# Middle stores of a one-core hybrid decoder step issued by GpSimd, g0 written in one transfer, and one round of background visits instead of three

## The chip, the cores and the metric

The kernel runs on one core of a Trainium2 chip. The metric is the device time of one execution in microseconds. The engines are TensorE (PE), VectorE (DVE), ScalarE (ACT), GpSimd (POOL) and SyncE (SP). Each works through its own instructions in order. Loads and stores run on 16 DMA engines; an instruction on SP's, ACT's or POOL's queue issues them.

## The reference

One inference step of a two-layer decoder, for a prompt of 512 positions and a sample group of 8 sequences of 8 positions, 576 columns in all, model width 2048:

```
layer 0: h = rms_norm(x); q,k,v,z_a,b,c,h_in,z_b = split(h @ w_in_ab, 8)
  prompt attention: 8 heads x 128, three dilated causal windows merged
  sample attention: the same against a cache of 2048 keys and values per sequence
  mixer B: b * conv3(c * h_in);  y = concat(o_a * silu(z_a), o_b * silu(z_b)) @ w_out_ab
layer 1: u,z = split(rms_norm(x) @ w_in_c, 2)
  S5: 128 groups, 16 channels, 64 complex states, chunked scan, Re(C h) + D u
  y = gelu(y); y = y * sigmoid(y @ w_glu + b); out = x + (y * silu(z)) @ w_out_c
final rms_norm; new keys, values, conv and SSM states are outputs too
```

All arithmetic is fp32. Main products split both operands into a high and a low fp32r part and use three products of the four.

## The kernel before

**Main work.** There are 120 jobs in a fixed order: 0 to 23 the heads' q, k and v columns, 24 to 31 z_a, 32 to 63 the convolution's columns, 64 to 67 the output projection, 68 to 99 u and z, 100 to 115 the GLU, 116 to 119 the last projection. A job of the narrow kind (all but 64 to 67 and 116 to 119) has 96 main matmuls of 288 columns, in eight groups of 12. Weights come as 512 KB tiles `w` from SP's queue; ACT makes the high part `wh`, DVE the low part `wl` (`wl = w - wh`), and the matmuls write PSUM tiles `mm`, of which there are two.

**Background work.** Everything else is a Python generator, a *thread*. A thread yields what its next step waits for (an engine, tiles, free buffers, a condition) and goes on when it is resumed. The order of all instructions is written out once, when the program is built, by a planner: class `Clock` adds up an estimated time for each engine and each DMA, and `could` says whether a thread's next step would be ready by that estimate. Before each group of 12 main matmuls `between` calls `step`; in this text that is a **visit**. A visit first lets evacuations of PSUM go on (`evacs`, as far as they can), and then goes round the threads in order of priority, each one step, up to three rounds. A step for an engine that is planned over 3.5 us ahead is not taken. Where the main work can go no further (`until`), `force` resumes the thread that is ready first, with no main matmuls beside it. Since an engine keeps its order, an instruction that was planned too early holds up all that stand behind it.

**The stretches.** `prompt_heads` runs the eight heads one after another, 24 steps and a condition each; a head can begin when its three jobs are done. Beside it `ssm_setup` prepares the state-space layer and starts `ssm_x` (16 chunks: load tiles E and B, DVE makes X, store to bx_scr) and `ssm_c` (16 chunks: transposes tx, tile XY, DVE makes Cs, matmuls gp with B0, stores to cs_scr, and for each two chunks g0 in tile gsb to gz_scr). X, Cs and gsb have one buffer each. `heads_done` is asked from job 24 on, and from job 29 on it is forced (`until(heads_done)` in `hook2`). Then `open_sample` starts the sample attention: `near_load` and `far_load` bring cache tiles kv and kf (512 KB each), `sample_far` works on DVE with kf, and `sample_near` goes through four pairs of sequences, 54 steps a pair: 20 for keys (tkn, sps), 11 to the softmax (nw, tf, tp), 21 for values (os), and two for the output. When it is done, `fill_o` splits the stored columns of o_scr for the output projection; `hook3` forces that at job 64. In layer 1 `v_phase`, `scans`, `y_phase`, `gelus` and `final_states` run beside jobs 68 to 99, and `fill_y` (38 steps) must be done for job 100.

**Queues around the change.** Loads are issued on SP. Stores of the middle of the program are issued on ACT, next to ACT's activations: the heads' k, v and q, oa_scr and o_scr, bx_scr, cs_scr, gz_scr, the convolution states, h_scr, z_scr and the final SSM states. An issue waits on the issuing queue until its tile is complete. POOL has some memsets, the copies into qz (for each sample pair) and into HV (for each scan), and two small loads at the start. The planner counts 370 ns for an issue on any engine and a landing 3200 ns after the data.

Of the kernel before, what the change touches and what calls it, by code (L numbers as in the profile page):

```python
# [10 lines left out]
F32 = mybir.dt.float32  # L11
# [7 lines left out]
P = 128  # L19
D = 2048  # L20
KT = 16
NP = 512
# [7 lines left out]
G = 128  # L30
GC = 16
ST = 64
# [46 lines left out]
class Clock:  # L79
# [91 lines left out]
    def op(self, eng, op, a, k):  # L171
        aps = [(n, x) for n, x in list(enumerate(a)) + list(k.items()) if hasattr(x, "tensor")]
        outs = [x for n, x in aps if n in (0, "out", "accum_out")]
        ins = [x for n, x in aps if n not in (0, "out", "accum_out")]
        by = "DMA" if op == "dma_start" else eng
        t = max([self.when(x, False, by) for x in ins] + [self.when(x, True, by) for x in outs])
        if op == "dma_start":
            at = max(self.t[eng], t) + 370
            self.t[eng] = at
            n = int(np.prod(outs[0].shape))  # L180
            run = min(self.packets(x, x.tensor.name in self.row) for x in outs + ins)
            self.dma = max(self.dma, at) + n / run * (5 + 0.2 * run) / 16
            end = max(self.dma, at) + 3200
        else:
            at = max(self.t[eng], t + 60)
            two = op != "memset" and sum(x.tensor.name in self.sbuf for x in ins) > 1
            shared = two if eng == "DVE" else eng == "POOL" and op != "memset"
            if shared:
                at = max(at, self.port)
            end = at + self.cost(eng, op, outs, ins)  # L190
            if eng == "PE":
                fast = op == "matmul" and ins[0].dtype == F32R
                if fast and not self.exact:
                    end += 85
                self.exact = fast
            self.t[eng] = end
            if shared:
                self.port = end
            if eng == "PE":
                end += 170  # L200
        for x in ins:
            self.note(x, end, False, by)
        for x in outs:
            self.note(x, end, True, by)
# [74 lines left out]
def hybrid_step(tc, I, O):  # L279
# [26 lines left out]
    _, cp = pools.open("const")  # L306
    _, wp = pools.open("wstream")
# [26 lines left out]
    e_scr = dr.tile([T, G, P], F32, name="e_scr")  # L334
    b_scr = dr.tile([GC, G, P], F32, name="b_scr")
    q_scr = dr.tile([64, 1024], F32, name="q_scr")
    gz_scr = dr.tile([G, GC, 240], F32, name="gz_scr")
    m0_scr = dr.tile([P, G, P], F32, name="m0_scr")
    bx_scr = dr.tile([P, G, P], F32, name="bx_scr")
    cs_scr = dr.tile([P, G, P], F32, name="cs_scr")  # L340
# [94 lines left out]

    def step():
        evacs()
        for _ in range(3):
            again = False
            for th in list(bg):  # L440
                if th in bg and could(th, 3500.0):
                    run(th)
                    again = True
                    evacs()
            if not again:
                return
# [452 lines left out]
    def ev_za(h, ps):  # L899
        yield W("DVE", ps)  # L900
        zs, th, gt = evt(2), evt(3), evt(0)
        mul(half(zs), ps, half(rstd))
        yield W("ACT", zs, flag=lambda: h in za_in)
        act(th, zs, AF.Tanh, scale=0.5)
        ob = za_in.pop(h)
        yield W("DVE", th, ob)
        stt(gt, th, 1.0, zs, ALU.add, ALU.mult)
        stt(ob, ob, 0.5, gt[:, 0:NP], ALU.mult, ALU.mult)
        yield W("ACT", ob)
        act(gs[:, h, :], gt[:, NP:])  # L910
        ACT.dma_start(out=o_scr[h, :, 0:NP], in_=ob)

    def load_oa():
        for h in range(NH):
# [14 lines left out]
    def prompt_head(h):  # L929
# [51 lines left out]
            PE.transpose(tk[:, i, :], k[:, i * P:(i + 1) * P], ident)  # L981
        kt_ = pp.tile([P, 4, P], F32, name="ktok", tag="PT", bufs=2)
        act(kt_, tk)
        ACT.dma_start(out=kout[:, h, :].rearrange("(i p) d -> p i d", p=P), in_=kt_)
        yield W("ACT", S[0][1])
        ex(0)
        yield w_qk(1)
# [8 lines left out]
            PE.transpose(tv_[:, i, :], v[:, i * P:(i + 1) * P], ident)  # L996
        vt_ = pp.tile([P, 4, P], F32, name="vtok", tag="vtok", bufs=2)
        act(vt_, tv_)
        ACT.dma_start(out=vout[:, h, :].rearrange("(i p) d -> p i d", p=P), in_=vt_)
        yield w_qk(2)  # L1000
        qk(2)
        yield W("DVE", S[1][0])
# [8 lines left out]
        sq = pp.tile([64, 2, P], F32, name="sq", tag="sq", bufs=1)  # L1011
        act(sq, tq[:, 0:2, :])
        DVE.tensor_copy(vs[:, h * P:(h + 1) * P], tq[:, 2, :])
        ACT.dma_start(out=q_scr[:, h * P:(h + 1) * P], in_=sq[:, 0, :])
        ACT.dma_start(out=ksout[:, h, :], in_=sq[:, 1, :])
        ACT.dma_start(out=vsout[:, h, :], in_=vs[:, h * P:(h + 1) * P])
        yield w_tr(0)
        tr(0)
        yield w_qk(3)
# [23 lines left out]
        yield W("ACT", o, slot=[(pp, "PT", 1)])  # L1043
        ob = pp.tile([P, NP], F32, name="ob", tag="PT", bufs=2)
        act(ob, o)
        ACT.dma_start(out=oa_scr[h], in_=ob)
        hs["done"] = h + 1


# [2 lines left out]
    def ssm_setup():  # L1052
# [15 lines left out]
        DVE.memset(pw[:, 0, 0, :], 1.0)  # L1068
        DVE.memset(pw[:, 0, 2, :], 1.0)
        for a in range(2):  # L1070
            SP.dma_start(out=gz_scr[:, :, 56 * a:56 * a + 56], in_=pw[:, 0, 1, 0:56].unsqueeze(1).to_broadcast([P, GC, 56]))
        yield W("ACT", lam, stp)
        lr, li = lam[:, 0, :], lam[:, 1, :]
        act(stp, stp, AF.Exp)
# [118 lines left out]
    def ssm_x(sp):  # L1193
        for c in range(G // CH):
            g0 = c * CH
            yield W("SP", e_scr, b_scr, slot=[(sp, "E8", 1), (sp, "B8", 1)])
            E = sp.tile([P, CH, 2, ST], F32, name="E8", tag="E8", bufs=1)
            B = sp.tile([P, CH, 2, ST], F32, name="B8", tag="B8", bufs=1)
            SP.dma_start(out=E.rearrange("p g a s -> p (g a s)"), in_=e_scr[:, g0:g0 + CH, :]
                         .rearrange("t g p -> t (g p)").unsqueeze(1).to_broadcast([T, GC, CH * P]))  # L1200
            SP.dma_start(out=B.rearrange("p g a s -> p (g a s)"), in_=b_scr[:, g0:g0 + CH, :]
                         .rearrange("k g p -> k (g p)").unsqueeze(0).to_broadcast([T, GC, CH * P]))
            er, ei, br, bi = E[:, :, 0, :], E[:, :, 1, :], B[:, :, 0, :], B[:, :, 1, :]
            yield W("DVE", E, B, slot=[(sp, "X8", 1)])
            X = sp.tile([P, CH, 2, ST], F32, name="X8", tag="X8")
            for a, (p, q, f) in enumerate(((br, bi, sub), (bi, br, add))):
                tb = sp.tile([P, CH, ST], F32, name="tb8", tag="tb8")
                mul(tb, ei, q)
                mul(X[:, :, a, :], er, p)
                f(X[:, :, a, :], X[:, :, a, :], tb)  # L1210
                if a == 0:
                    yield W("DVE")
            yield W("ACT", X)
            ACT.dma_start(out=bx_scr[:, g0:g0 + CH, :], in_=X.rearrange("p g a s -> p g (a s)"))
        st_["x"] = True
        ssm_end()

    def ssm_c(sp, B0, PWT):
# [13 lines left out]
        for c in range(G // CH):  # L1232
# [24 lines left out]
            for q in range(2):  # L1257
                for gi in range(4):
# [1 line left out]
                    PE.matmul(gp[32 * gi:32 * gi + 32, q, :], B0[:, (g0 + g) * GC:(g0 + g) * GC + 32],  # L1260
                              Cs[:, g, 0:8, :].rearrange("p t k -> p (t k)"), start=True, stop=True,
                              tile_position=(0, 32 * gi))
            ACT.dma_start(out=cs_scr[:, g0:g0 + CH, :], in_=Cs[:, :, 1:9, :].rearrange("p g t k -> p g (t k)"))
            if c % 2 == 0:
                gs_["t"] = sp.tile([P, 4, P], F32, name="gsb", tag="gsb")
            gsb = gs_["t"]
# [2 lines left out]
                stt(gsb[:, 2 * (c % 2) + q, 0:GC], eye, dsk[:, 2 * c + q:2 * c + q + 1], gp[:, q, 0:GC], ALU.mult, ALU.add)  # L1269
            if c % 2:  # L1270
                yield W("ACT", gsb)
                for gi in range(4):
                    ACT.dma_start(
                        out=gz_scr[(c - 1) * CH:(c + 1) * CH].rearrange("(q gi) k j -> gi k q j", gi=4)[gi][:, :, 112:240],
                        in_=gsb[32 * gi:32 * gi + GC])
        st_["c"] = True
        ssm_end()

# [6 lines left out]
    def m0_expand():  # L1285
        for t in range(T):
            yield W("SP", flag=lambda: cnt["i"] >= 4 * 64 + 6 * t)
            SP.dma_start(out=m0_scr[t * GC:(t + 1) * GC],
                         in_=gz_scr[:, :, GC * t:GC * t + P].rearrange("g k j -> k g j"))


    cvs = {}
# [1 line left out]
    def ev_conv(n, ps):  # L1294
# [32 lines left out]
        elif kind == 2:  # L1327
# [6 lines left out]
            nv = pp.tile([32, P], F32, name="ncv", tag="ncv")  # L1334
            act(nv[0:18, :], tl[0:18, :])
            js = slice(j * P, (j + 1) * P)
            ACT.dma_start(out=O["conv_p"][0, 0][:, js], in_=nv[0:2, :])
            ACT.dma_start(out=O["conv_s"][0].rearrange("b i f -> (b i) f")[:, js], in_=nv[2:18, :])
        else:
            yield W("DVE", ps)  # L1340
            zs, th, ob = evt(0), evt(1), evt(2)
# [9 lines left out]
            if "t" in Bt:  # L1351
                yield from split_B(8 + j, ob)
            else:
                ACT.dma_start(out=o_scr[8 + j], in_=ob)
                stored.append(8 + j)

    stored = list(range(8))
# [80 lines left out]
    def sample_near():  # L1438
# [115 lines left out]
            DVE.tensor_scalar(out=osb, in0=o, scalar1=st[:, 2:3], scalar2=None, op0=ALU.mult)  # L1554
            yield from sample_out(pr, osb)
        yield W("ACT", sa["oS"])
        ACT.dma_start(out=o_scr[0:8, :, NP:].rearrange("h p n -> p h n"), in_=sa["oS"])
        sa["done"] = True

    def open_sample():  # L1560
# [30 lines left out]
    def ev_out0(part, g, acc, tiles):  # L1591
# [15 lines left out]
        for i, n, h, x in got:  # L1607
            yield W("ACT", h)
            act(x, h, AF.Square, accum_out=ssqa[0:n, 4 * i + g:4 * i + g + 1])
            h1["xc"] += 1  # L1610
            ACT.dma_start(out=h_scr[i * P:i * P + n, g * 512:(g + 1) * 512], in_=h)

    def joined(ps):

# [81 lines left out]
    def ev_z(n, ps):  # L1696
        yield W("DVE", ps)
        zs, th = evt(1), evt(2)
        mul(half(zs), ps, half(h1["rstd"]))
        yield W("ACT", zs)  # L1700
        act(th, zs, AF.Tanh, scale=0.5)
        yield W("DVE", th)
        stt(th, th, 1.0, zs, ALU.add, ALU.mult)
        yield W("ACT", th)
        ACT.dma_start(out=z_scr[n], in_=th)

    w_c = I["w_in_c"][0]
    add_jobs(w_c, [m * P for m in range(16)], actA, ev_u)
# [170 lines left out]
    def final_states():  # L1879
# [3 lines left out]
        for src, re_out, im_out in outs:  # L1883
# [3 lines left out]
            f = sp.tile([G, P], F32, name="fo", tag="sn", bufs=3)  # L1887
            act(f, t)
            yield W("ACT", f)
            ACT.dma_start(out=re_out, in_=f[:, 0:ST])  # L1890
            ACT.dma_start(out=im_out, in_=f[:, ST:P])
        ss["fo"] = True

    def open_ssm():
# [327 lines left out]
```

## Time and profile before

| | us |
|---|---|
| median of 3 runs | 2350.19 |
| lowest, highest | 2349.2, 2360.9 |
| profiled execution | 2350.44 |
| its span, first to last instruction | 2348.5 |

Mean granted clock of TensorE over the span: 0.974. In the profile, busy times and idle times are in microseconds. In a list of instructions, "x" is their number. An idle time names the engine's own gap before the instruction and, after "<-", what ended it. A "q" behind an engine's name (ACTq) means its queue's own instruction, such as the issue of a DMA. PEclk is the granted share of TensorE's full clock of 2.4 GHz; the other level is 1.2 GHz. A DMA share of 1.0 means that all 16 DMA engines are busy.

### The profile page before, as it was taken

Reading aid. Unit: us, or ns where it says so; the run is one execution under the profiler, and the core shown is the slowest. Engines: PE = TensorE matmul, PEld = TensorE weight load, DVE = VectorE, ACT = ScalarE, POOL = GpSimd, SP = SyncE. Lnnn points to the kernel's source line nnn. Section 1 sums busy time; section 2 is a strip of 40 time slices with the busy share of each in tenths; the row PEclk is TensorE's granted clock in tenths of the full one; section 3 lists DMA queues with packets and bytes.
Section 4 is the critical chain, followed back from the end, with each engine's and each line's share of the span. In section 5 each row is a group of like instructions: output and inputs, shape, how many; then the busy total and the mean of one; then the engine's idle time right before and its main releaser. Section 6 shows DMA issues by size and latency. Waiting matters only on the chain.

```text
span 2348.5 us, 38368 instructions
## 1 busy us (share of the span) xinstructions
PE 2206.3 (94%) x15581; PEld 2034.7 (87%) x15581; DVE 1264.8 (54%) x2380; ACT 695.8 (30%) x1400; POOL 13.5 (1%) x52
## 2 busy tenths in 40 slices
PE   6998888899888989999999999999999999999997
PEld 5997777798676868899988789999999999998885
DVE  3776676746575644343323334787996534443333
ACT  4543333332121222232223333222233322332222
POOL 0000000000000000000000000000000000000000
PEclk9999999999898999999999999999999999999999
DMA  6466666659999987732246535465555643338212
GB/s 170 112 170 179 176 174 179 177 180 254 261 284 216 287 227 217 212 113 80 84 153 187 158 112 158 128 204 156 175 168 163 188 120 102 107 110 214 88 63 81
DMA packets 421796, 386.62 MB, mean 165 GB/s; under 512 B 34620, under 2 KB 349860, under 8 KB 420276
## 3 DMA queue, kind: packets, MB, share of 16 engines
q1 hardware_dynamic: 369552, 340.63, 52.6%
q10 hardware_dynamic: 52004, 43.53, 6.0%
q8 instruction: 122, 2.00, 0.4%
q14 instruction: 54, 0.44, 0.1%
q0 software_dynamic: 64, 0.02, 0.0%
HBM read 329.22 MB, written 63.28 MB: 167 GB/s over the span
## 4 chain that ended last, share of the span: by engine, by line
PE 70%; DMA 15%; DVE 9%; ACT 3%; issue 2%; SPq 1%; ACTq 0%; DVEq 0%
PE mm L215 59%; DMA kv<-cache_win_v 4%; DMA kf<-cache_win_k 3%; PE mms L215 3%; DVE m L215 2%; PE yps L215 2%; DMA B<-b_scr 2%; DMA out_win_k_p<-ktok 1%; PE os L215 1%; DVE wl L215 1%; DMA oa<-oa_scr 1%; SPq L215 1%; DMA w<-w_in_ab 1%; PE vps L215 1%; PE tkn L215 1%
## 5 line engine op out<-in xcount | busy, mean ns | idle before, releaser
L215 PE MATMUL mm<-a_hi,wh 128*128 128x288 f32 x3072 | 695.1, 308 | 5.7 <-ACT a_hi L215 5.7
L215 DVE TENSOR_TENSOR wl<-w,wh 128x512 fp32r<-128x512 f32 x576 | 392.3, 688 | 545.4 <-ACT wh L215 529.0
L215 PE MATMUL mm<-a_hi,wl 128*128 128x288 f32 x3072 | 666.5, 299 | 12.6 <-DVE wl L215 12.6
L215 PE MATMUL mm<-a_lo,wh 128*128 128x288 f32 x3072 | 666.3, 299 | 0.4 <-DVE a_lo L215 0.3
L215 ACT ACTIVATE wh<-w 128x512 fp32r<-128x512 f32 x576 | 357.3, 627 | 719.0 <-PE mm L215 363.5
L215 PEld LDWEIGHTS mm<-a_hi,wh 128*128 128x128 f32 x3072 | 502.5, 193 | 43.9 <-issue 28.1
L215 PEld LDWEIGHTS mm<-a_hi,wl 128*128 128x128 f32 x3072 | 502.4, 192 | 13.6 <-DVE wl L215 13.6
L215 PEld LDWEIGHTS mm<-a_lo,wh 128*128 128x128 f32 x3072 | 503.4, 192 | 1.2 <-DVE a_lo L215 1.2
L215 PE MATMUL mm<-y_hi,wh 128*128 128x288 f32 x512 | 109.7, 296 | 0.0
L215 PE MATMUL mm<-y_lo,wh 128*128 128x288 f32 x512 | 109.6, 296 | 0.0
L215 PE MATMUL mm<-y_hi,wl 128*128 128x288 f32 x512 | 109.6, 296 | 0.0
L215 PE MATMUL mm<-wh,a_hi 128*128 128x512 f32 x256 | 100.0, 391 | 1.9 <-DVE Y L215 1.9
L215 DVE TENSOR_TENSOR kf<-kf,qr 128x1024 f32<-128x1024 f32 x48 | 58.6, 1221 | 79.3 <-DMA kf<-cache_win_k 79.3
L215 PE MATMUL mm<-wh,o_hi 128*128 128x512 f32 x256 | 100.5, 393 | 0.0
L215 PE MATMUL mm<-wl,o_hi 128*128 128x512 f32 x256 | 99.7, 389 | 0.0
L215 PE MATMUL mm<-wh,o_lo 128*128 128x512 f32 x256 | 99.7, 389 | 0.0
L215 PE MATMUL mm<-wh,a_lo 128*128 128x512 f32 x256 | 99.6, 389 | 0.0
L215 PE MATMUL mm<-wl,a_hi 128*128 128x512 f32 x256 | 99.6, 389 | 0.0
L215 PEld LDWEIGHTS mm<-y_hi,wh 128*128 128x128 f32 x512 | 82.5, 189 | 0.0
L215 PEld LDWEIGHTS mm<-y_lo,wh 128*128 128x128 f32 x512 | 82.5, 189 | 0.0
L215 PEld LDWEIGHTS mm<-y_hi,wl 128*128 128x128 f32 x512 | 82.5, 189 | 0.0
L215 DVE TENSOR_TENSOR m<-HV,AT 64x256 f32<-64x256 f32 (+5 forms) x120 | 67.8, 565 | 3.6 <-ACT HV L215 1.2
(290 smaller groups left out, 2343.9 us busy)
## 6 DMA issues: line engine op xcount, KB each, us to landing
w<-w_in_ab SPq DMA_DIRECT2D x128, 512.0 KB
kv<-cache_win_v SPq DMA_DIRECT2D x80, 512.0 KB
w<-w_in_c SPq DMA_DIRECT2D x64, 512.0 KB
kf<-cache_win_k SPq DMA_DIRECT2D x48, 512.0 KB
kv<-cache_win_k SPq DMA_DIRECT2D x32, 512.0 KB
w<-w_out_ab SPq DMA_DIRECT2D x32, 512.0 KB
w<-w_glu SPq DMA_DIRECT2D x32, 512.0 KB
w<-w_out_c SPq DMA_DIRECT2D x32, 512.0 KB
```

The costliest lines, as they stand in the source:

```text
L215: r = f(*a, **k)
```

## The change

Stores that ACT issued are issued by POOL, with the planner counting 900 ns in place of 370 ns for an issue on POOL. The stores of y_scr and those of the last outputs stay on ACT. gz_scr has 32 rows a group in place of 16, so that the 128 partitions of gsb go out in one transfer and not in four; readers take the first 16. `step` goes round the threads once.

```diff
-            at = max(self.t[eng], t) + 370
+            at = max(self.t[eng], t) + (370 if eng != "POOL" else 900)
...
-    gz_scr = dr.tile([G, GC, 240], F32, name="gz_scr")
+    gz_scr = dr.tile([G, 32, 240], F32, name="gz_scr")
...
     def step():
         evacs()
-        for _ in range(3):
+        for _ in range(1):
...
-        ACT.dma_start(out=kout[:, h, :].rearrange("(i p) d -> p i d", p=P), in_=kt_)
+        POOL.dma_start(out=kout[:, h, :].rearrange("(i p) d -> p i d", p=P), in_=kt_)
...
-            ACT.dma_start(out=bx_scr[:, g0:g0 + CH, :], in_=X.rearrange("p g a s -> p g (a s)"))
+            POOL.dma_start(out=bx_scr[:, g0:g0 + CH, :], in_=X.rearrange("p g a s -> p g (a s)"))
...
-            ACT.dma_start(out=cs_scr[:, g0:g0 + CH, :], in_=Cs[:, :, 1:9, :].rearrange("p g t k -> p g (t k)"))
+            POOL.dma_start(out=cs_scr[:, g0:g0 + CH, :], in_=Cs[:, :, 1:9, :].rearrange("p g t k -> p g (t k)"))
...
-                for gi in range(4):
-                    ACT.dma_start(
-                        out=gz_scr[(c - 1) * CH:(c + 1) * CH].rearrange("(q gi) k j -> gi k q j", gi=4)[gi][:, :, 112:240],
-                        in_=gsb[32 * gi:32 * gi + GC])
+                POOL.dma_start(out=gz_scr[(c - 1) * CH:(c + 1) * CH].rearrange("(q gi) k j -> (gi k) q j", gi=4)[:, :, 112:240],
+                               in_=gsb)
```

The same move from ACT to POOL is made for the stores of o_scr, vout, q_scr, ksout, vsout, oa_scr, conv_p, conv_s, h_scr, z_scr and the final SSM states. The two readers of gz_scr take `0:GC` of its rows.

## Rows read from the trace of the kernel before

**Rows 1.** The page, part 1: busy time of each engine.

```profile
PE 2206.3 (94%) x15581; PEld 2034.7 (87%) x15581; DVE 1264.8 (54%) x2380; ACT 695.8 (30%) x1400; POOL 13.5 (1%) x52
```

**Rows 2.** Windows, main matmuls alone: length, busy (count), PEclk, DMA share, GB/s.

```profile
482.90:503.60 20.70, 17.06 (x109) 14.91 (x109) 1.15 (x2) 0.00 (x0) 1.00 0.27 75
516.00:972.30 456.30, 304.99 (x2058) 286.42 (x2057) 16.33 (x29) 0.00 (x0) 0.95 0.96 252
801.00:895.00 94.00, 58.79 (x397) 54.22 (x396) 3.14 (x6) 0.00 (x0) 0.98 0.93 254
972.30:1183.50 211.20, 211.20 (x1582) 210.90 (x1583) 12.64 (x24) 0.00 (x0) 1.00 0.35 103
1017.00:1119.40 102.40, 102.40 (x768) 102.26 (x767) 6.32 (x12) 0.00 (x0) 1.00 0.30 86
1811.40:1920.50 109.10, 107.25 (x804) 107.28 (x805) 6.04 (x8) 0.00 (x0) 1.00 0.54 155
```

**Rows 3.** Windows: length, PE, PEld, DVE, ACT, POOL busy, PEclk, DMA share, GB/s.

```profile
180.00:240.00 60.00, 50.59 (x391) 47.43 (x391) 40.38 (x87) 19.42 (x47) 0.00 (x0) 0.94 0.66 170
...
420.00:480.00 60.00, 51.07 (x396) 48.03 (x385) 39.52 (x82) 20.06 (x46) 3.01 (x9) 0.94 0.62 174
...
600.00:660.00 60.00, 54.09 (x352) 38.15 (x352) 32.63 (x37) 10.08 (x18) 0.00 (x0) 0.91 1.06 291
```

**Rows 4.** Waits of PE, 170 to 500 us: total, times, longest.

```profile
PE tq L215 <- ACT XY L215: 20.0, 3, 7.0
PE pt L215 <- ACT S L215: 9.9, 5, 3.1
PE s L215 <- DVE S L215: 8.6, 2, 4.6
```

**Rows 5.** Waits of ACT, 170 to 500 us: total, times, longest.

```profile
ACT S L215 <- DMA gz_scr<-gsb: 23.4, 2, 11.9
ACT wh L215 <- DVE X L215: 22.5, 6, 6.9
```

**Rows 6.** Timeline around 180 us: start, length, engine, instruction, idle before it.

```profile
178.63 11.25 ACTq L215 DMA_DIRECT2D gz_scr<-gsb  x4
...
189.93 0.40 ACT L215 ACTIVATE S<-S,st 128x128 f32<-128x128 f32 x1 [11.89 <-DMA gz_scr<-gsb]
...
190.90 0.64 PE L215 MATMUL tq<-ident,qk 128*64 128x128 f32 x2 [7.05 <-ACT XY L215]
```

**Rows 7.** Timeline around 255 us.

```profile
252.31 0.69 DVE L215 TENSOR_TENSOR tb<-E,B 128x512 f32<-128x512 f32 x1 [4.21 <-DMA B<-b_scr]
...
254.72 1.65 PE L215 MATMUL s<-qk 128*128 128x384 f32 x2 [4.57 <-DVE S L215]
...
258.20 4.33 ACTq L215 DMA_DIRECT2D gz_scr<-gsb  x4
```

**Rows 8.** Groups of PE, 505 to 980 us: count, busy, mean ns, idle before.

```profile
L215 PE MATMUL os<-kv,PTs 128*32 128x512 f32 x320 | 57.1, 625 | 10.5 <-DMA kv<-cache_win_v 10.5
L215 PE MATMUL tkn<-ident,kv 128*128 128x128 f32 x256 | 34.7, 280 | 0.4 <-DMA kv<-cache_win_k 0.4
L215 PE MATMUL sps<-KT,qz 128*32 128x128 f32 x512 | 19.7, 276 | 6.2 <-DVE KT L215 6.2
L215 PE MATMUL tp<-ident,Ss 128*128 128x128 f32 (+1 forms) x44 | 6.0, 288 | 2.6 <-ACT Ss L215 2.6
```

**Rows 9.** Waits of PE and DVE, 505 to 980 us.

```profile
PE mm L215 <- DVE wl L215: 12.0, 3, 8.2
...
DVE kf L215 <- DMA kf<-cache_win_k: 79.3, 24, 15.5
```

**Rows 10.** Groups of POOL, whole span: a DMA that it issues.

```profile
L215 POOL DMA_DIRECT2D vr<-ssm_norm x1 | 0.6, 619 | 0.2 <-issue 0.2
```

**Rows 11.** DMA issues by line: queue, count, KB, median us to landing.

```profile
vr<-b_glu POOLq DMA_DIRECT2D x1, 8.0 KB, 9.2
```

**Rows 12.** The chain that ended last, in order: start, length, what.

```profile
1530.98 3.79 DMA u_scr<-uu
```

More of the change, by code (lines that the diff above doesn't have):

```diff
@@ L910, in ev_za @@
         act(gs[:, h, :], gt[:, NP:])
-        ACT.dma_start(out=o_scr[h, :, 0:NP], in_=ob)
+        POOL.dma_start(out=o_scr[h, :, 0:NP], in_=ob)
     def load_oa():
@@ L998, in prompt_head @@
         act(vt_, tv_)
-        ACT.dma_start(out=vout[:, h, :].rearrange("(i p) d -> p i d", p=P), in_=vt_)
+        POOL.dma_start(out=vout[:, h, :].rearrange("(i p) d -> p i d", p=P), in_=vt_)
         yield w_qk(2)
@@ L1013, in prompt_head @@
         DVE.tensor_copy(vs[:, h * P:(h + 1) * P], tq[:, 2, :])
-        ACT.dma_start(out=q_scr[:, h * P:(h + 1) * P], in_=sq[:, 0, :])
-        ACT.dma_start(out=ksout[:, h, :], in_=sq[:, 1, :])
-        ACT.dma_start(out=vsout[:, h, :], in_=vs[:, h * P:(h + 1) * P])
+        POOL.dma_start(out=q_scr[:, h * P:(h + 1) * P], in_=sq[:, 0, :])
+        POOL.dma_start(out=ksout[:, h, :], in_=sq[:, 1, :])
+        POOL.dma_start(out=vsout[:, h, :], in_=vs[:, h * P:(h + 1) * P])
         yield w_tr(0)
@@ L1045, in prompt_head @@
         act(ob, o)
-        ACT.dma_start(out=oa_scr[h], in_=ob)
+        POOL.dma_start(out=oa_scr[h], in_=ob)
         hs["done"] = h + 1
@@ L1070, in ssm_setup @@
         for a in range(2):
-            SP.dma_start(out=gz_scr[:, :, 56 * a:56 * a + 56], in_=pw[:, 0, 1, 0:56].unsqueeze(1).to_broadcast([P, GC, 56]))
+            SP.dma_start(out=gz_scr[:, 0:GC, 56 * a:56 * a + 56], in_=pw[:, 0, 1, 0:56].unsqueeze(1).to_broadcast([P, GC, 56]))
         yield W("ACT", lam, stp)
@@ L1288, in m0_expand @@
             SP.dma_start(out=m0_scr[t * GC:(t + 1) * GC],
-                         in_=gz_scr[:, :, GC * t:GC * t + P].rearrange("g k j -> k g j"))
+                         in_=gz_scr[:, 0:GC, GC * t:GC * t + P].rearrange("g k j -> k g j"))
     cvs = {}
@@ L1336, in ev_conv @@
             js = slice(j * P, (j + 1) * P)
-            ACT.dma_start(out=O["conv_p"][0, 0][:, js], in_=nv[0:2, :])
-            ACT.dma_start(out=O["conv_s"][0].rearrange("b i f -> (b i) f")[:, js], in_=nv[2:18, :])
+            POOL.dma_start(out=O["conv_p"][0, 0][:, js], in_=nv[0:2, :])
+            POOL.dma_start(out=O["conv_s"][0].rearrange("b i f -> (b i) f")[:, js], in_=nv[2:18, :])
         else:
@@ L1353, in ev_conv @@
             else:
-                ACT.dma_start(out=o_scr[8 + j], in_=ob)
+                POOL.dma_start(out=o_scr[8 + j], in_=ob)
                 stored.append(8 + j)
@@ L1556, in sample_near @@
         yield W("ACT", sa["oS"])
-        ACT.dma_start(out=o_scr[0:8, :, NP:].rearrange("h p n -> p h n"), in_=sa["oS"])
+        POOL.dma_start(out=o_scr[0:8, :, NP:].rearrange("h p n -> p h n"), in_=sa["oS"])
         sa["done"] = True
@@ L1610, in ev_out0 @@
             h1["xc"] += 1
-            ACT.dma_start(out=h_scr[i * P:i * P + n, g * 512:(g + 1) * 512], in_=h)
+            POOL.dma_start(out=h_scr[i * P:i * P + n, g * 512:(g + 1) * 512], in_=h)
     def joined(ps):
@@ L1704, in ev_z @@
         yield W("ACT", th)
-        ACT.dma_start(out=z_scr[n], in_=th)
+        POOL.dma_start(out=z_scr[n], in_=th)
     w_c = I["w_in_c"][0]
@@ L1889, in final_states @@
             yield W("ACT", f)
-            ACT.dma_start(out=re_out, in_=f[:, 0:ST])
-            ACT.dma_start(out=im_out, in_=f[:, ST:P])
+            POOL.dma_start(out=re_out, in_=f[:, 0:ST])
+            POOL.dma_start(out=im_out, in_=f[:, ST:P])
         ss["fo"] = True
```

## Prediction

> **What bounds the kernel now.** I read the page first. TensorE (PE) is busy for 94% of the span [rows 1], so the time is the matmul work plus what PE idles and what a lowered clock costs. Two things can be had: gaps and clock, nothing else. The undisturbed pace comes next: 768 main matmuls in 102.40 us, 0.1333 us each, 1.60 us for the 12 between two visits, at a full clock [rows 2]. Two stretches fall short of it. In the five 60 us slices from 180 to 480 us PE has some 10 us of gaps each, and the granted clock is 0.94 in the first and the last; the slice at 600 us shows 0.91 with the DMA engines full (share 1.06) [rows 3].
>
> The first stretch is the attention heads beside the state-space set-up. The waits of PE there say who ends the gaps: 20.0 us before tq, released by ScalarE (ACT), 9.9 us before pt, also ACT, 8.6 us before s, released by VectorE (DVE) [rows 4]. Then the waits of ACT: 23.4 us for the gz_scr stores in two pieces, 22.5 us before wh for DVE's X [rows 5]. The timeline shows what these are. Four gz stores hold ACT's queue for 11.25 us, its next exponential starts after 11.89 us idle, and PE's tq, behind that, has idled 7.05 us [rows 6]. At 258 us the same four took 4.33 us [rows 7]. So issuing a store can stop ACT, and through wh and the bg PSUM tiles it stops PE. The 22.5 us are bx_scr stores, whose issue waits in ACT's order until DVE has made X. The third kind isn't ACT's: DVE idles 4.21 us for the B load and PE 4.57 us behind it [rows 7].
>
> The second stretch is the sample attention, 516 to 972 us. Its 2058 main matmuls at 0.1333 us need 274.4 of 456.3 us [rows 2]; the three largest background groups are 57.1 + 34.7 + 19.7 = 111.5 us [rows 8]. That leaves 70.4 us for six smaller groups of at most 6.0 us each [rows 8] and for loss, so the loss is between 34 and 70 us. DVE waits 79.3 us there for kf loads, the longest 15.5 us, and PE 12.0 us for wl behind DVE [rows 9]: with full DMA engines loads land later than the order written out by hand supposes.
>
> **Part 1, stores to GpSimd (POOL).** 194 issues leave ACT, 170 come to POOL (32 gz become 8). They are off ACT's order, with their waits for ACT's and DVE's results. The 20.0 us before tq go, and half of the 9.9 before pt: -20 and -5. The 8.6 us stay, as the E and B loads stay on SP with the same estimate. Clock: at 0.94 an eighth of a slice ran at the 1.2 GHz level, which costs 3.6 us in 60 us, 18 us for five slices [rows 3]; when the gaps go, half should return: -9.
>
> What it adds: POOL's issue takes 0.62 us where the trace has one [rows 10], 170 x 0.62 = 105 us on an engine that is busy for 13.5 [rows 1]. That is an 8 KB transfer; the trace has no large one. Bounds: the same 0.62 us whatever the size, or, if all of it is per 512 B piece (16 there, 1024 in a cs_scr store), 40 us for a cs_scr store and 640 us for its sixteen. I take the low end, nearest to the only row, and keep the other as a rival. Landing took 9.2 us at the program's start [rows 11] against 3.79 us for a store from SP [rows 12]. It matters where a tile has one buffer: X8, Cs, gsb, 40 stores. Their next writer comes most of a chunk later, five visits or more (8 us of main matmuls and the background beside them), so I count 0; uncovered, it is up to 40 x 5.4 = 216 us. Queued behind a waiting store on POOL are the qz and HV copies and memsets, within the 13.5 us; PE's sps and DVE's scans wait for them.
>
> Against this part speaks the Trainium skill, DMA: Bandwidth & Descriptors, section Issuing engines are not separate DMA queues: issuing from more engines saves only the sequencer's issue time, usually small beside the transfer. By it the -20 and -5 fall away and the sum below ends 25 us higher. The trace disagrees: the issue itself took 11.25 us for four [rows 6].
>
> **Part 2, gz.** One transfer for four: three issues fewer, twice the bytes (16 unread rows a group are written too), 8 x 128 KB more. Nothing waits for it until job 64: 0.
>
> **Part 3, one round in place of three.** Between two groups of 12 main matmuls each background thread now takes one step. The trace shows how far more is used: the last head took its 24 steps within 109 main matmuls, 9 visits; the third sample pair its 54 in 397, 33 visits [rows 2]. Hence a head now needs 25 visits and some misses, and gets 24 (three jobs). A lag of about 2 a head is allowed by the buffers of q, k and v, so eight heads end near visit 240, past the 232 where line `until(heads_done)` forces the rest without main matmuls. A forced step costs at least (20.7 - 109 x 0.1333) / 24 = 0.26 us and at most 20.7 / 24 = 0.86 us, since with main matmuls between them they took no longer [rows 2]. 12 steps at the upper end: +10.
>
> The sample attention opens about 30 visits later and takes 216 steps and some 20 misses where it had 171 visits. This is what I expect most of: the same bytes spread over a third more main work, so that the DMA share falls from 0.96 to below 0.85 and kf comes in time. 0.30 with idle engines stands behind it [rows 2], unused. Of the loss, 34 to 70 us, middle 52, I take two thirds: -34. Bounds: 0 if loads are late by their latency and not by the load of the engines, -70.
>
> The price is room at the end. 1582 main matmuls, 132 visits, lie between the sample's end and job 64 [rows 2]. Now 30 + 65 are used up by delay and steps and about 46 by fill_o: 141. Nine forced steps, at 0.9 us (between 0.26 and 1.74, which is 94.0 / 54 of the third pair): +8. At the GLU, 67 visits [rows 2] stand against 38 of fill_y and about 20 of later outputs: +2. The scans are held by DVE and its 3.5 us limit, not by rounds: 0.
>
> **Sum.** -20 - 5 - 9 - 34 + 10 + 8 + 2 = -48 us. The profiled execution took 2350.44 us with a span of 2348.5, the median of the runs is 2350.19; so 2350.4 - 48 = **2302 us**.
>
> **Rivals.**
> (a) *One round starves the threads.* If every fifth step finds its data not ready, a head needs 30 visits, the heads 40 more, forced at 0.86: 34 us; the sample needs 43 more, all past job 64, at 1.74: 75 us. 2302 + 34 + 75 = 2411. It decides from about 27 visits a head, or a sample attention that ends after job 60. For: DVE waits in both stretches [rows 7, 9]. Against: the last head's 24 steps in 9 visits, most found ready at once.
> (b) *The late loads stay the bound.* ACT is free, but DVE still stops at B and kf, wl is late as before. Only -20 - 5 + 20 is left: 2345, no change. For: 79.3 us of DVE wait have nothing to do with ACT.
> (c) *Stores land late and hold their buffers.* The move doesn't take the wait away; DVE meets it at X8, Cs and gsb. A quarter of the 216 us reaches PE: 2302 + 54 = 2356. It decides from a landing over some 10 us. The trap of GpSimd's descriptors in SBUF — State Buffer of the Trainium skill, section SBUF: two separate sides, would cause it: a DVE copy in a two-port mode locks GpSimd out while it writes descriptors. No trace here shows it yet, and the DVE work beside the stores has two inputs, as tb from E and B [rows 7], which is not that form.
> (d) *More comes back.* All of the clock and of the loss: -9 - 36 more, 2257.
>
> **How the numbers follow.** Forecast, 2270 to 2338: 0.50. (d) 0.10. (b) 0.18. (c) 0.08. (a) 0.14. About 0.5% (12 us) is what a measurement can tell from no change. Faster by more: 0.50 + 0.10 = 0.60. Within: (b) and half of (c), 0.22. Slower: (a) and half of (c), 0.18. The range leaves out the far part of (d) and most of (a): 2250 to 2372.
>
> **What would show it.** Right: no ACT gap over 5 us with a store behind it between 170 and 500 us, and tq no longer in PE's waits; heads and sample over later in main matmuls, DMA share nowhere at 1.0, kf waits of DVE under half of 79.3 us, clock near 1.00 in the sample. Wrong: forced steps, seen as runs of head or sample matmuls without main ones near jobs 29 and 64; DVE waits on bx_scr, cs_scr or gz_scr stores; POOL issues of several us; a new PE wait before the w_out matmuls.

## The result and the profile after

| | us |
|---|---|
| before, median of the runs beside it | 2349.69 |
| after, median of 4 runs (2278.94 to 2286.27) | 2280.78 |
| ratio, with its 95% interval | 0.9711 (0.9661 to 0.9762) |
| profiled execution after, and its span | 2286.27, 2284.4 |
| mean granted clock, before and after | 0.974, 0.986 |

The change makes the kernel 2.9% faster. The forecast was 2302 us, with a range from 2250 to 2372. The page, part 1, answers to [rows 1]:

```profile
PE 2183.2 (96%) x15581; PEld 2016.4 (88%) x15581; DVE 1263.7 (55%) x2380; ACT 690.1 (30%) x1400; POOL 117.9 (5%) x226
```

PE does the same 15581 matmuls in 23 us less, and idles 41 us less. The windows after (length, PE, PEld, DVE, ACT, POOL busy, PEclk, DMA share, GB/s), against [rows 3]:

```profile
180.00:240.00 60.00, 56.87 (x442) 54.15 (x441) 46.80 (x101) 21.71 (x50) 9.39 (x14) 0.97 0.66 181
...
420.00:480.00 60.00, 52.93 (x414) 50.38 (x414) 42.33 (x91) 19.16 (x46) 11.43 (x17) 0.97 0.75 204
...
600.00:660.00 60.00, 57.79 (x415) 48.80 (x415) 37.19 (x50) 14.59 (x27) 3.29 (x11) 1.00 1.07 242
```

All three slices have more PE work and a higher clock. The DMA share of the third is what it was. The waits of PE from 170 to 500 us (total, times, longest) begin with these, and tq, first in [rows 4], is not among them at all:

```profile
PE gp L215 <- DVE Cs L215: 8.1, 8, 1.5
PE pt L215 <- ACT S L215: 4.0, 1, 4.0
```

Where the 64.1 us of the two spans lie is found by cutting both traces at the same work: the first main matmul of a job, and the last matmul `o` of the heads. The second cut needs a correction: one round moves heads' steps to later visits, so in the changed kernel the last `o` came at visit 228 (511.2 us) and not at 201 (503.5 us). 27 visits at the undisturbed 1.60 us [rows 2] are an estimated 43.2 us of main work that changed sides. A cut at a fixed job instead (jobs 9 to 24 take 305.8 and 246.8 us, jobs 24 to 64 take 701.0 and 693.6) counts the moved steps as a gain ahead of the cut and a loss behind it; the expectations below still use such cuts.

| stretch | before | after | gain |
|---|---|---|---|
| start to job 9 | 177.1 | 177.2 | -0.1 |
| job 9 to the last `o` of the heads | 326.4 | 334.0, with 43.2 more main work | 35.5 |
| from there to job 64 | 680.4 | 606.4, with 43.2 less | 30.8 |
| output projection, jobs 64 to 67 | 214.4 | 217.3 | -2.9 |
| jobs 68 to 99 | 522.2 | 515.3 | 6.9 |
| GLU | 204.8 | 204.8 | 0 |
| last projection | 209.9 | 215.9 | -6.0 |

### The profile page after: what moved, and what is told of

Read it like the earlier page. It is cut to its first block, busy times and chain, and to the rows that moved or that the text cites. A ratio compares the mean times of both kernels' runs of the same rounds, so it can differ in the third digit from the quotient of the medians.

```text
span 2284.4 us, 38430 instructions
## 1 busy us (share of the span) xinstructions
PE 2183.2 (96%) x15581; PEld 2016.4 (88%) x15581; DVE 1263.7 (55%) x2380; ACT 690.1 (30%) x1400; POOL 117.9 (5%) x226
## 5 line engine op out<-in xcount | busy, mean ns | idle before, releaser
L215 PEld LDWEIGHTS mm<-a_hi,wh 128*128 128x128 f32 x3072 | 494.3, 191 | 60.6 <-issue 40.3
L215 PEld LDWEIGHTS mm<-a_lo,wh 128*128 128x128 f32 x3072 | 498.4, 190 | 8.1 <-DVE a_lo L215 8.1
L215 DVE TENSOR_TENSOR kf<-kf,qr 128x1024 f32<-128x1024 f32 x48 | 58.6, 1221 | 63.7 <-DMA kf<-cache_win_k 63.7
L215 ACT ACTIVATE S<-S,st 128x128 f32<-128x128 f32 (+3 forms) x64 | 35.0, 557 | 140.6 <-DVE st L215 140.4
```

The lines of the kernel that those rows point to most:

```text
L215: r = f(*a, **k)
```

## The experiments

Call P the stores on GpSimd (with the planner's 900 ns for an issue there), G the one gz transfer, R the one round. With the kernel before, the first seven kernels make all combinations; further ones take single causes apart. The two columns at the right are gains by the same correction, from the start to the last `o` of the heads and in the third stretch above, each from one profiled execution. Kernels below that are the same program up to job 116 (with and without gf first) differ in these columns by up to 3.7 us, so differences of that size mean nothing. The profiled execution before took 2350.44 us, 1 to 8 us more than the medians of before beside these runs, so the columns together show some us more than the ratios.

| kernel | median, us | ratio to before (95%) | heads | sample |
|---|---|---|---|---|
| G | 2295.84 | 0.9803 (0.9777 to 0.9830) | 45.4 | 11.5 |
| P | 2311.38 | 0.9851 (0.9809 to 0.9892) | 44.8 | 3.9 |
| P + G | 2307.33 | 0.9865 (0.9833 to 0.9897) | 42.9 | -0.9 |
| R | 2284.66 | 0.9760 (0.9730 to 0.9790) | 34.4 | 25.2 |
| R + G | 2276.53 | 0.9711 (0.9674 to 0.9748) | 49.3 | 25.6 |
| R + P | 2284.94 | 0.9750 (0.9711 to 0.9788) | 47.9 | 19.9 |
| P + G + R, the change | 2280.78 | 0.9711 (0.9661 to 0.9762) | 35.5 | 30.8 |
| G and three small stores | 2339.63 | 0.9983 (0.9963 to 1.0004) | 9.3 | 5.8 |

### One part undone, one part alone

**P + G.** The changed kernel with three rounds.

```diff
-        for _ in range(1):
+        for _ in range(3):
```

> The changed kernel with its three rounds of background visits back; the stores stay on GpSimd and gz stays one transfer. Theory (the stores' issue and their waits stopped ScalarE, and that made TensorE's gaps in the heads): jobs 9 to 24, which fell from 305.8 to 246.8 us, stay at 260 us or less, tq and the 5 us ScalarE gaps stay away, and the sample stretch is as before; the time is about 2350 - 45 = 2305 us. Rival 1 (one round does it: spreading keeps the loads and the chains of three engines apart): jobs 9 to 24 go back to 295 us or more, about 2345 us. Rival 2 (the two need each other): 2330 us, jobs 9 to 24 near 280 us.

2307.33 us, jobs 9 to 24 in 264.0 us: the theory's time, with a little more than its 260 us in those jobs. So the heads' gain needs no R.

**R.** The kernel before with one round.

```diff
-        for _ in range(3):
+        for _ in range(1):
```

> The kernel before with one round of background visits in place of three, and nothing else of the change. Theory: the gz and bx stores still stop ScalarE, so the tq gaps stay; jobs 9 to 24 take 290 to 306 us; later the sample work is spread and gains the 7 us that the changed kernel shows for jobs 24 to 64 and 7 us for jobs 68 to 99: about 2336 us. Rival 1 (one round carries the gain): about 2290 us, jobs 9 to 24 under 260 us. Rival (a) of the prediction, threads starved while ScalarE is still stopped: forced steps before job 29 and job 64, over 2360 us.

2284.66 us, and the theory failed: it wanted the tq gaps to stay. The waits of PE from 170 to 500 us of this kernel begin like this, without tq:

```profile
PE gp L215 <- DVE Cs L215: 12.7, 10, 4.2
PE pt L215 <- ACT S L215: 3.6, 2, 2.8
```

Jobs 9 to 24 took 262.3 us, near Rival 1's 260, and nothing was starved, though the heads ended only at visit 232, the limit. Two rounds were not measured.

**G.** The kernel before with gz as one transfer, from ACT.

```diff
-                for gi in range(4):
-                    ACT.dma_start(out=gz_scr[...]...[gi][:, :, 112:240],
-                                  in_=gsb[32 * gi:32 * gi + GC])
+                ACT.dma_start(out=gz_scr[...].rearrange("(q gi) k j -> (gi k) q j", gi=4)[:, :, 112:240],
+                              in_=gsb)
```

> The kernel before with gz as one transfer in place of four, still issued by ScalarE, and three rounds. Four issues held ScalarE for 11.25 us at most and 4.33 us in another place. If the block is the number of issues, one takes a quarter: the 20.0 us of TensorE before tq fall to about 5, time about 2335 us. Rival: if an issue is held by what the queues still have to take (128 KB each, the larger one twice a smaller), one transfer of twice the bytes holds ScalarE about as long: 2345 to 2350 us, tq still 10 us or more in TensorE's waits.

2295.84 us. Both expectations were too high: three issues less in eight places give 46 us, more than P and G together (35). Around 178 us ACT now goes on 0.1 us after the issue, with the XY that released tq late in [rows 4] (timeline, as [rows 6]):

```profile
177.91 0.62 ACTq L215 DMA_DIRECT2D gz_scr<-gsb  x1
178.60 0.37 ACT L215 ACTIVATE XY<-tx,sgn 128x128 f32<-128x128 f32 x1 [1.22 <-DVE S L215]
```

Three different edits had each taken away tq's waits for ACT. That asked for a cause which all three touch.

### What the four issues waited for

The line of [rows 6] groups four issues in 11.25 us. The single records show that each took 0.31 to 0.66 us, with 4.66, 2.06 and 2.92 us between them. They also name the semaphore by which each transfer tells that it has landed, and for some issues one of these as what the issue waits for:

```
before: queue, issue begins, transfer        tells by   waits for
SP    176.33  E<-e_scr                        102
SP    176.98  B<-b_scr                        104        106
ACT   177.06  bx_scr<-X                       103
SP    177.61  cn<-c_re                        106
ACT   178.07  out_win_k_p<-ktok               105
ACT   178.63  gz_scr<-gsb                     107
ACT   183.95  gz_scr<-gsb                     102        102
ACT   186.35  gz_scr<-gsb                     103        103
ACT   189.57  gz_scr<-gsb                     105        105
```

In this program all transfers of SP and ACT tell by eight semaphores (100, 102 to 107, 116), which they take in turn; POOL's have eight others (108 to 115). An issue waits until the transfer that had its semaphore last has landed. The second gz issue waits for the E load of 7.6 us earlier, the third for the bx store, the fourth for the kout store. Some of these waits are instructions of their own just before the issue, which the list leaves out. With them, from 170 to 500 us, ACT waited 35.3 us like this before, 23.8 with R, 9.0 with R + G, 3.6 with G and 0 with P, where it issues no transfer there.

So the trace agrees with a sentence of the Trainium skill, DMA: Bandwidth & Descriptors, section Anatomy of one DMA — SWDGE (gpsimd) path: a DMA engine never waits on a semaphore, the issuing sequencer does, before it hands the transfer over. The section is about transfers from GpSimd; the trace shows it for ACT's queue. What follows on that queue, ACT's exponentials here, stands behind it.

**G and three small stores.** If that is the cause, bytes don't matter and the number of issues does.

```diff
                 ACT.dma_start(out=gz_scr[...]..., in_=gsb)
+                for k in range(3):
+                    ACT.dma_start(out=dm_scr[3 * c + k:3 * c + k + 1], in_=gsb[k:k + 1, 0, :])
```

> The kernel with gz as one transfer (2296 us) with three stores of 512 B from the same tile behind it on ScalarE, so that the number of issues is that of the kernel before and the bytes stay those of one transfer. Nothing else is changed; the three rows go to a scratch tensor that nobody reads. New theory (an issue waits for the landing of the transfer eight issues earlier, so the number in a row counts and the bytes don't): the waits of 5 us between the issues and TensorE's idle time before tq come back, jobs 9 to 24 at 290 us or more, time 2330 to 2350 us. Rival (the four stores were slow for their pieces or bytes): three 512 B issues cost 3 x 0.4 us on ScalarE and no more, 2296 to 2302 us.

2339.63 us: three rows of 512 B undo G's gain. Timeline of ACT, and PE's tq behind it:

```profile
177.05 0.75 ACTq L215 DMA_DIRECT2D gz_scr<-gsb  x1
182.03 5.17 ACTq L215 DMA_DIRECT2D dm_scr<-gsb  x3
187.25 0.40 ACT L215 ACTIVATE S<-S,st 128x128 f32<-128x128 f32 x1 [10.73 <-DMA out_win_k_p<-ktok]
...
188.22 0.64 PE L215 MATMUL tq<-ident,qk 128*64 128x128 f32 x2 [5.83 <-ACT XY L215]
```

The three small issues begin at 182.03, 184.19 and 186.98 and wait for semaphores 102, 103 and 104, much as the second to fourth gz store did (102, 103 and 105). ACT's waits for a semaphore's earlier transfer are back at 32.7 us. The rival, pieces or bytes, is out.

One thing is not separated. All these edits also change the order that the planner writes out: with G, PE's instructions stand in another order from 181 us on, and the three small stores bring the order of before back, instruction for instruction. Directly behind the gz issues lie tq's 20.0 us and, at the lower clock just after each, some 5 us more, so 25 of the 45 us that G gains in the heads. The rest, s's 8.6 us among it, went with the order and the number of issues together.

**R + G, P, R + P.** The remaining combinations, from the same few lines.

> The kernel before with one round and gz as one transfer; all stores stay on ScalarE and SyncE. New theory: the transfers that SyncE and ScalarE issue share eight completion semaphores in turn, and an issue waits until the transfer that had its semaphore eight issues earlier has landed; four gz issues in a row met the E, B, bx and kout transfers that were still under way (in the trace of before the second gz issue waits for the semaphore of the E load issued 7.6 us earlier). One round or one gz transfer each take that away, so the stores' move is not needed: jobs 9 to 24 at 245 to 258 us, the sample stretch as with one round alone (684 us), w_out at 214.4 instead of 217.3 us; time 2265 to 2282 us. Rival: with one round, the stores' issue on ScalarE is the next limit and the move to GpSimd is worth the 15 us that jobs 9 to 24 show between one round alone (262.3) and the changed kernel (246.8): 2290 us or more.

> The kernel before with the stores moved to GpSimd, with four gz stores and three rounds. New theory: GpSimd's transfers have eight semaphores of their own, so the four gz stores wait for nothing of SyncE's and stop no ScalarE work: the same as with gz in one transfer, 2300 to 2312 us, jobs 9 to 24 at 258 to 270 us. Rival 1 (the gain of the stores with gz in one transfer, 2307 us, was gz's alone, as gz alone has 2296): 2335 us or more. Rival 2 (GpSimd's issues are the new queue): four gz issues more in a chunk hold the bx and cs stores back by 4 x 0.77 us and DVE waits for X and Cs: 2320 us.

> The changed kernel with gz in four transfers again, all from GpSimd, one round. New theory: gz's number no longer counts when the stores have their own semaphores and leave ScalarE: as the changed kernel, 2276 to 2288 us. Rival: 24 more issues of 0.77 us on GpSimd delay the chain through cs and gz: 2295 us or more.

2276.53, 2311.38 and 2284.94 us, each within or at the edge of what the semaphores let expect. P alone takes the stall away with four gz stores: they are off ACT's queue, and by the records none of POOL's stores there waited for an earlier transfer of its semaphore. R + G without P has the ratio of the whole change: **moving the stores is worth nothing that the time shows once gz is one transfer**. With three rounds it costs (G 0.9803, P + G 0.9865, intervals just apart). In the output projection the four kernels with stores on POOL take 217.3 to 218.7 us, all others 214.4 to 214.5. There PE waits two or three times 0.9 us before jp for ACT's js; why was not tried.

### The last projection

Kernels with one round lose 2 to 7 us there. DVE (first line) and PE of the changed kernel:

```profile
2108.30 1.29 DVE L215 TENSOR_TENSOR Y<-Y,gf 128x512 f32<-128x512 f32 x2 [4.68 <-DMA gf<-final_norm]
...
2110.84 0.79 PE L215 MATMUL mm<-wh,a_hi 128*128 128x512 f32 x1 [3.56 <-DVE Y L215]
```

The load of gf stands behind the row loads of Y, which wait for each other's semaphores. **gf first**, on R + G:

```diff
+        SP.dma_start(out=fo["g"], in_=I["final_norm"].unsqueeze(0).to_broadcast([P, D]))
         for i in range(5):      # the row loads of Y
...
-        SP.dma_start(out=fo["g"], in_=I["final_norm"].unsqueeze(0).to_broadcast([P, D]))
```

> One round and gz as one transfer, all stores on ScalarE (2276.5 us), with the load of gf issued ahead of the rows of Y in the last projection. All kernels with one round show one gap of TensorE of 3.6 to 4.6 us there, behind a VectorE wait of 5.7 us for gf, and the last projection takes 213.9 to 217.1 us where it took 209.9. Theory (gf's load lies last behind 24 row loads, each of which waits for the transfer eight issues earlier): the gap goes, the last projection takes 209 to 212 us, time 2270 to 2274 us. Rival: gf, 1 MB, then delays the rows of Y, and another gap of the same size comes before mm behind Y: 2275 to 2280 us.

2269.17 us, 0.9664 (0.9637 to 0.9690); the last projection took 209.5 in place of 216.9 us, and DVE no longer waits for gf. As the theory has it, with a time just under its range.

### What the sample stretch still loses

After the change DVE still waited for kf from 505 to 1080 us (total, times, longest; [rows 9] has 79.3), and with R + G 55.9:

```profile
DVE kf L215 <- DMA kf<-cache_win_k: 63.7, 24, 11.5
```

**kf from GpSimd, kf from ScalarE, kf left out,** all on R + G.

```diff
-                yield W("SP", slot=[(pp, "kf", 1)], flag=...)
+                yield W("POOL", slot=[(pp, "kf", 1)], flag=...)
...
-                SP.dma_start(out=sa["kf"][n], in_=far_ap(ck, b, t))
+                POOL.dma_start(out=sa["kf"][n], in_=far_ap(ck, b, t))
```

The planner counts 900 ns for GpSimd's issue here too; the kernel with ScalarE names ACT in both lines.

> One round and gz as one transfer (2276.5 us), with the 48 kf loads of the sample attention issued by GpSimd in place of SyncE. They leave SyncE's order (which waits for fs, kv and weight buffers in turn) and its eight semaphores. Theory A (the loads are late because SyncE's one order holds them behind each other's buffers): jobs 24 to 64 fall from 687.7 by 15 us or more, VectorE's waits for kf halve, time 2255 to 2262 us. Theory B (what is late is late because the DMA engines are full, share 1.02 to 1.08): the same within 6 us, 2270 to 2283 us, DMA share as before. Rival: GpSimd's transfers land late and DVE's wait for kf grows: 2290 us or more.

> As the kernel with the kf loads from GpSimd, but from ScalarE: they leave SyncE's order and stay among the eight completion semaphores that SyncE and ScalarE share. Theory A1 (SyncE's one order, in which a load that waits for its buffer holds all behind it): jobs 24 to 64 at 660 to 672 us as with GpSimd (664), time 2255 to 2266 us. Theory A2 (the eight semaphores: 12.6 us of SyncE's waits from 520 to 1000 us are for a semaphore's earlier transfer): no gain, 684 to 692 us, time 2272 to 2280 us. Rival: an issue that waits for its kf buffer stops ScalarE's own work (its exponentials and the KT copies), and more is lost than won: 2285 us or more, with ScalarE gaps behind kf.

For the third, the first three tiles are used again:

```diff
-                sa["kf"][n] = pp.tile([P, 1024], F32, name="kf", tag="kf", bufs=3)
-                SP.dma_start(out=sa["kf"][n], in_=far_ap(ck, b, t))
+                if n < 3:
+                    kf3.append(pp.tile([P, 1024], F32, name="kf", tag="kf", bufs=3))
+                    SP.dma_start(out=kf3[n], in_=far_ap(ck, b, t))
+                sa["kf"][n] = kf3[n % 3]
```

> One round and gz as one transfer (2276.5 us), but only the first three of the 48 kf loads are made and their tiles are used again, so 45 loads of 512 KB of the sample attention are left out (the scores of the far keys are then not the reference's); all instructions of VectorE and TensorE stay. Theory B (full DMA engines): the share in the slices from 540 to 720 us falls below 0.95, TensorE's gaps there shrink, and jobs 24 to 64 fall from 687.7 by 15 us or more: 2255 to 2262 us. Theory A (the order of SyncE's issues): the 45 loads are out of that order too, so as much. Rival C (TensorE waits for chains of ScalarE and VectorE and not for loads): under 6 us less, 2270 to 2278 us.

| kernel | median, us | ratio to before (95%) | jobs 24 to 64 | sample gain |
|---|---|---|---|---|
| R + G | 2276.53 | 0.9711 (0.9674 to 0.9748) | 687.7 | 25.6 |
| kf from GpSimd | 2257.31 | 0.9624 (0.9588 to 0.9659) | 664.0 | 50.5 |
| kf from ScalarE | 2255.17 | 0.9612 (0.9588 to 0.9635) | 663.9 | 50.6 |
| 45 kf loads left out | 2237.88 | 0.9527 (0.9497 to 0.9558) | 649.3 | 67.4 |

Moving 48 loads to another queue, with every byte kept, gains 24 us in the stretch. PE's and DVE's instructions stand in the same order as in R + G, so it isn't the planner's order. It is the same from ScalarE, which shares SP's eight semaphores, so it is SP's order and not the semaphores (A1). The 12.6 us in that expectation are too low: with the wait instructions counted in, SP waited from 520 to 1000 us 22.6 us for its semaphores' earlier transfers with R + G, and still 19.4 us with kf on ScalarE, which has the whole gain. ScalarE did stop at these loads: each issue took some 0.54 us, but it stood idle up to 9.5 us before one, and the time shows none of that. What SP waited for between 540 and 840 us, with kf on SP and then on POOL, shows the order:

```profile
SPq L215 <- DVE fs L215: 21.8, 9, 8.0
```

```profile
SPq L215 <- DVE fs L215: 0.5, 1, 0.5
```

A kf load waits for its buffer, which DVE's sum fs gives free, and until then holds up the kv and w loads behind it. With kf on another queue, DVE's waits for kf tiles are gone (GpSimd's kernel; what is left under kf is two waits for qr):

```profile
DVE kf L215 <- DMA qr<-q_scr: 6.4, 2, 4.7
```

The windows from 600 to 660 us, R + G, then kf from GpSimd, then kf left out:

```profile
600.00:660.00 60.00, 54.53 (x360) 41.74 (x360) 32.64 (x39) 8.45 (x15) 0.00 (x0) 0.94 1.07 246
```

```profile
600.00:660.00 60.00, 56.83 (x403) 45.85 (x402) 32.49 (x44) 8.43 (x14) 5.50 (x16) 0.97 1.06 290
```

```profile
600.00:660.00 60.00, 59.73 (x464) 49.39 (x463) 43.25 (x61) 11.67 (x23) 0.00 (x0) 1.00 0.89 261
```

The first two have the same DMA share and move 246 and 290 GB/s. Only without the bytes does the share of this slice fall below 1, and PE idles 0.6 us in all from 505 to 1100 us. The gain is well over the 15 us that both theories asked for. So about 67 us of the stretch hung on these loads: R + G gave back 25, the order of the queue another 25, and some 17 go with the 45 loads themselves. Theory B can claim this last part at most, since without these loads the planner also writes another order from the sample stretch on.

**kf from GpSimd and gf first.** The two edits above together, on R + G.

> One round, gz as one transfer, the kf loads issued by GpSimd (2257.3 us) and gf ahead of the rows of Y. If the two places don't touch each other, the sum: the last projection 209.5 in place of 211.7 us, jobs 24 to 64 at 664 us, time 2250 to 2256 us, below all others. Rival: they meet in the final stretch (the order of loads moves again): 2257 to 2262 us.

2253.98 us, 0.9601 (0.9575 to 0.9627), last projection 209.6 us, jobs 24 to 64 in 668.3 us where 664 was expected. That is 1.2% under the changed kernel, intervals apart; from kf on GpSimd or on ScalarE alone it can't be told.

## Why the prediction was right, and where it was not

**The forecast** held in sign and in size: 48 us forecast, 64 measured between the profiled executions. The places of the two large terms were right; the reasons beside them were right only in part, and that both came out within 4 us of the forecast is in part luck.

**Heads: -20 - 5 - 9.** The sum, 34, measured 35.5. By the records PE idled 49.3 us in that stretch before and 19.7 after, and lost 12.9 and 5.9 us at the lower clock while it was busy: 7.0 for the 9. Of the idle time tq's 20.0 went as put. Of pt's 9.9 only 1.2 went, s's 8.6 for DVE, which were to stay, went, and gp's wait for Cs rose from 4.2 to 8.1. From 170 to 515 us, where the heads end after (PE, then DVE):

```profile
PE pt L215 <- ACT S L215: 8.7, 2, 4.7
```

```profile
DVE tb L215 <- DMA B<-b_scr: 44.9, 13, 8.2
```

Both pt waits, 4.0 us at 447 and 4.7 us at 504, stand behind DVE steps that waited for a B load. DVE's 44.9 us there were 18.5 before; they are 11.1 with R + G and 23.6 with R + P, which idle PE only 11.5 and 10.5 us in the heads and gain 48 to 49. Why B comes later in the changed kernel is not shown. Without that the heads might have given some 13 us more, so that the 34 came out is in part luck.

The reason for the 20 and the 5 was half wrong. That "the issue itself took 11.25 us for four" is the step that failed: the issues took 0.31 to 0.66 us each, the rest was the wait for earlier transfers of the same semaphores. So the text credited part 1 with what either of the other two parts gives too, and set part 2 at 0, which alone is worth 46 us.

**The rule weighed against part 1.** Beside these runs the Trainium skill, DMA: Bandwidth & Descriptors, section Issuing engines are not separate DMA queues, by which issuing from more engines saves only the sequencer's issue time, was nearer than the prediction said: with gz in one transfer, the move of the stores saved nothing that the time shows. But the runs show a second thing that the rule leaves out, the order of a queue: with the kf loads on ScalarE another queue gave 21 us.

**Forced steps: +10 and +8.** Neither came. The heads ended at visit 228, forecast near 240, under the 232 of job 29: a head lagged less than the two visits allowed for. The sample attention took its 216 steps in 251 visits, where 236 were counted, and ended at visit 487. It thus left 25 visits for the 46 of `fill_o`; still PE had no gap at job 64, and the last of these steps, on ACT and DVE, ran beside that job, to 1158 us. The price of 0.9 us was taken from steps with matmuls of their own; here lies most of the 16 us that the forecast was short.

**Sample: -34.** 30.8 measured, and the loss before, put at 34 to 70, was some 67 by the kernel without kf loads. The reason again failed in part: the DMA share did not fall below 0.85. It stood at 1.02 to 1.08 in four of the five slices from 540 to 840 us, and kf waits fell to 63.7, not under half of 79.3. Loads were held up by their queue's order as much as by full engines, which rival (b) came close to saying.

**POOL: 0.** Its busy time went from 13.5 to 117.9 us, 104 for 105 forecast. The open question of a store's price by its pieces is settled at the low end (the tile's own view, shortest, median and longest in ns; then the list of issues from 170 to 500 us, with KB and median us to landing):

```profile
L215 POOL DMA_DIRECT2D cs_scr<-Cs x16: 900/907/930, 187.7 to 471.7; - x16
```

```profile
cs_scr<-Cs POOLq DMA_DIRECT2D x16, 512.0 KB, 6.6
bx_scr<-X POOLq DMA_DIRECT2D x15, 512.0 KB, 9.5
```

Landing took a median of 9.5 us for bx and 11.8 at the longest, about the 10 us from which rival (c) was to decide. The buffers mostly allowed it: DVE waited 3.1 us for cs_scr stores and never for bx_scr or gz_scr ones, and gp's waits for Cs are all that PE can show of it. Its cause would be the lock that the Trainium skill, SBUF — State Buffer, section SBUF: two separate sides, describes: GpSimd can't write descriptors while a DVE copy in a two-port mode holds their shared port. No store from POOL shows it: all sixteen cs issues took 900 to 930 ns, and no other kind spreads by more than 50 ns.

**After job 64: +2.** Net 2.0, by chance: 2.9 and 6.0 lost and 6.9 gained, none of them foreseen. Rival (a) was out: no thread starved.

## What to carry to other kernels

When a group of DMA issues holds up an engine, look at the single issues and at what each waits for: a few semaphores taken in turn make a burst of small stores wait for large transfers that have nothing to do with it, and one transfer in place of four can be worth as much as another engine. A load that waits for its buffer stops all loads behind it on its queue, so streams that wait for different consumers belong on different queues, and a DMA share near 1 doesn't prove that the engines can move no more (242 to 291 GB/s here at 1.06 and 1.07). When an edit moves background work in time, cut the traces at the end of that work and correct for the main work moved, or gain and loss are booked to the wrong stretch.

## What was not expected of the hardware

A store from GpSimd took 0.90 to 0.93 us of its time for the 512 KB of cs_scr, 0.54 to 0.56 us for the 512 KB of bx_scr, against 0.62 us for 8 KB [rows 10], so size hardly counts in the issue; a kf load of 512 KB took 0.51 us there and 0.54 us on ScalarE. At the same DMA share (1.06 and 1.07) the engines moved 290 and 246 GB/s in the same stretch of two kernels; which transfers fell into it was not compared. Why R alone hides the 23.8 us that ACT still waits for semaphores is argued only from the wider spacing of the heads' steps; no run shows it by itself.
